# Sevenfold products in units of 512 columns: sums in PSUM banks, and two of four weight sums by accumulating loads

## The chip, the cores and the metric

The kernel runs on one core of one Trainium2 chip. The metric is the device time of one launch in microseconds. The kernel before took 1854.59 us (median of three runs, 1854.23 to 1855.96).

## The reference

Two layers of a decoder trunk, 512 tokens of 1024 channels. Each layer multiplies the normed rows by one wide input matrix, runs five branches (A sparse attention, B latent attention, C differential attention, D spatial gating, E attention into a memory), gates each branch output, projects it, and adds the five projections under a second gate. Cut to what the change touches:

```python
xn = rms_norm(h, norm_g[l])
(..., gates, merge) = jnp.split(xn @ w_in[l], offsets, axis=-1)
gates = gates.reshape(B, S, 5, 512)
merge = merge.reshape(B, S, 5, 1024)
mixed = functools.reduce(jnp.add, [
    sigmoid(merge[:, :, n]) * ((o * silu(gates[:, :, n])) @ w_branch[l, n])
    for n, o in enumerate(branches)])
h = h + mixed @ w_out[l]
```

`gates` of one branch is a product of 1024 x 512 weights with the 512 rows of xn, `merge` one of 1024 x 1024 weights.

## The kernel before, in words

**Arithmetic.** Every dense product is made three times: each operand is a rounded part h and a remainder l, and `three` (L484) adds hh, hl and lh in PSUM, one matmul each (L485 to L487). Weights come in by SyncE's loads into tiles `raw`, ScalarE writes the rounded part `wh` (L371, L402), VectorE or POOL the remainder `wl` (L373, L405). The rows are kept transposed in eight tiles `xh` and `xl`, one for each 128 channels, 512 tokens wide.

**Order of the work.** The kernel is written out by a plan: `ORDER` is a list of tokens, each of which puts units into the plan, and attention runs beside as generators that are advanced by `tick` after each group of matmuls. A unit calls `begin` for each weight granule: that issues the loads of the granules up to four ahead and starts the splits of the next ones; one step of splitting is put in at each `tick`. Instructions are then placed by the program's builder, so that neighbours in the code can change places on an engine.

**The seven stage.** After the token `xs` the last units of a layer (gates of A, merges of A, gates of C, merges of C) use seven products of half blocks in place of eight. The weight block of 1024 channels x 256 columns is cut into four blocks a11, a21 (first column half, upper and lower channels) and a12, a22, each 512 channels x 128 columns; the rows are cut into four as well, and `x_prep` makes their sums t1 to t4. A unit `unit_s` (L509) is 256 columns: it runs products "11", "t2", "t3", "t1", "22", "t4", "21" in that order, each 4 channel tiles x 3 matmuls of 128x256 into a PSUM bank of its own. VectorE adds these up into two tiles `st` (L528), seven times 128x256 a unit; ScalarE copies the first (L526). There are 12 such units a layer, and after each merge unit follows one branch product (24 matmuls of 512 columns, tiles `pm`).

**Weights of the seven stage.** `gseven` loads a unit's block as two `raw` tiles of 512 KB. `seven_steps` (L363) makes four sums of blocks on POOL (`comb`, L380, tiles `ws`, 128x512), and splits the seven operands: `wh` on ScalarE, `wl` on VectorE, the second operand's on POOL. `raw` has four buffers of its own.

**Gate and merge.** A gate unit ends with tanh on ScalarE (L1373), a multiply on VectorE (L1374), a multiply with the branch output on POOL (L1375) and the split into `yh`, `yl`. A merge unit ends with tanh (L1414), VectorE's multiply-add with the branch product (L1403) and POOL's addition into `acc` (L1411).

Of the kernel before, what the change touches and what calls it, by code (L numbers as in the profile page):

```python
# [40 lines left out]
WSB = True  # L41
STB = True
# [15 lines left out]
class Pace:  # L58
    """Interleaves side streams (attention) with the dense products as they are traced."""
# [68 lines left out]
class Granule:  # L128
    """Up to four 128-row blocks of 256 columns of a weight, split in two fp32r parts."""

    def __init__(self, parts, n, width=256, raws=1):
        self.parts, self.n, self.width, self.raws = parts, n, width, raws


def trunk(tc, d, out, taps=None):
# [43 lines left out]
    def f32(ap):  # L179
        return ap.bitcast(F32)  # L180
# [13 lines left out]
    # ---- input rows, small vectors, constants  # L194
# [59 lines left out]
    # ---- rotary tables  # L254
# [42 lines left out]
    def rope(eng, x, j, ct, st, outs=None):  # L297
        """x [128, 2, h, 2H], token tiles 2j and 2j+1; rotated in place or into outs."""
# [19 lines left out]
    # ---- differential lambdas  # L318
# [20 lines left out]
    # ---- long lived tiles  # L339
# [23 lines left out]
    def seven_steps(g):  # L363
        """Seven combinations of the four 512 x 128 blocks of a granule, split, in the order of their products."""
        r0, r1 = g.raw
        a11, a21, a12, a22 = (r[:, :, c * 128:(c + 1) * 128] for r in (r0, r1) for c in range(2))
        g.prod = []

        def put(src):
            h, lo = (z.rearrange("p (k c) -> p k c", k=4) for z in wtile())  # L370
            A.activation(h, src, AF.Copy)  # L371
            yield
            (G if len(g.prod) in GSET else V).tensor_tensor(out=lo, in0=src, in1=f32(h), op=ALU.subtract)  # L373
            g.prod.append((h, lo))
            yield

        def comb(x, y, op):
            o = (blk(F32, "ws") if WSB else pp.tile([128, 512], F32, tag="p", name="ws")).rearrange(
                "p (k c) -> p k c", k=4)
            G.tensor_tensor(out=o, in0=x, in1=y, op=op)  # L380
            return o
        yield from put(a11)
        s1 = comb(a21, a22, ALU.add)
        s2 = comb(s1, a11, ALU.subtract)
        yield from put(s2)
        yield from put(comb(a11, a21, ALU.subtract))
        yield from put(s1)
        yield from put(comb(a12, s2, ALU.subtract))
        yield from put(a22)
        yield from put(a12)  # L390

    def split_steps(g):
        if g.raws == 2:
            yield from seven_steps(g)
            return
        g.raw = g.raw[0]
        g.h, g.l = [], []
        for a in range(0, g.n, 2):
            b = min(a + 2, g.n)
            h, lo = (z.rearrange("p (k c) -> p k c", k=2) for z in wtile())  # L400
            raw, hv, lv = g.raw[:, a:b, :g.width], h[:, :b - a, :g.width], lo[:, :b - a, :g.width]
# [46 lines left out]
    def gseven(w, c0):  # L448
        def parts(*raws):
            return [(r, w[k0 * 128:(k0 + 4) * 128, c0:c0 + 256].rearrange("(k p) c -> p k c", p=128))  # L450
                    for r, k0 in zip(raws, (0, 4))]
        g = Granule(parts, 4, 256, 2)
        order.append(g)
        return g
# [29 lines left out]
    def three(o, ah, al, bh, bl, st, sp):  # L484
        T.matmul(o, ah, bh, start=st, stop=False)  # L485
        T.matmul(o, ah, bl, start=False, stop=False)  # L486
        T.matmul(o, al, bh, start=False, stop=sp)  # L487

    def unit_t(gs, kts, rh, rl, evac, n=512, ms=2):
        """[cols, tokens]: column tiles of 128."""  # L490
# [9 lines left out]
    def unit_n(gs, kts, lh, ll, evac, nt=4):  # L500
        """[tokens, cols]: token tiles in pairs, 256 columns."""
# [7 lines left out]
    def unit_s(g, xb, evac):  # L509
        """Transposed 256 columns by 512 tokens in seven products of half blocks instead of eight."""  # L510
        def run():
            begin(g)
            th = [blk(F32, "st0"), blk(F32, "st1")] if STB else [tr(name="st0"), tr(name="st1")]
            c11, c12, c21, c22 = (t_[:, a:a + 256] for t_ in th for a in (0, 256))
            uses = {"11": [(c11, None)], "t2": [(c22, c11)], "t3": [(c21, c22)], "t1": [(c12, c22), (c22, c21)],
                    "22": [(c12, c12)], "t4": [(c21, c21)], "21": [(c11, c11)]}
            for n, b in enumerate(uses):
                o = psm("s7")[:, :256]
                while len(g.prod) <= n:
                    split_some()  # L520
                for kt in range(4):
                    three(o, g.prod[n][0][:, kt], g.prod[n][1][:, kt], *xb(b, kt), kt == 0, kt == 3)
                    tick(3 * 256 * 0.43)
                for dst, other in uses[b]:
                    if other is None:
                        A.activation(dst, o, AF.Copy)  # L526
                    else:
                        V.tensor_tensor(out=dst, in0=o, in1=other, op=ALU.add)  # L528
            evac(th)
        plan.append(run)  # L530
# [13 lines left out]
    # ---- norm of rows into transposed parts  # L544
# [3 lines left out]
    def norm_rows(rows, ss, gname, l, hi, lo, step=600.0):  # L548
        """rows: [128, 1024] tiles with their sums of squares; writes hi/lo[k] [128, 128 * len(rows)]."""
# [27 lines left out]
    # ---- attention  # L577
# [27 lines left out]
    def pv_causal(o, terms):  # L605
        """terms(kb) -> list of (stationary, part of P)."""
# [8 lines left out]
    def attend(steps, scores, norm, trans, pv, pv_rows=None):  # L615
        """steps: list of (unit, i, last); software pipelined over the steps."""
# [46 lines left out]
    # ================= layers  # L663
# [20 lines left out]
    def layer(l, mm):  # L684
# [5 lines left out]
        # -- memory keys and values  # L690
# [18 lines left out]
        # -- e_q, transposed, one head per column tile  # L709
# [73 lines left out]
        # -- columns 512:1636 in natural layout  # L783
# [114 lines left out]
        # -- latent attention operands  # L898
# [116 lines left out]
        # -- sparse attention  # L1015
# [109 lines left out]
        # -- differential attention, two of its four heads at a time  # L1125
# [93 lines left out]
        # -- spatial gating  # L1219
# [106 lines left out]
        # -- combinations of the half blocks of the normed rows  # L1326
        def x_prep():
            S["t2"] = [c4(F32R, "t2").rearrange("p (k c) -> p k c", k=4) for _ in range(2)]
            for n in ("t3", "t4"):
                S[n] = [[blk(name=n).rearrange("p (k c) -> p k c", k=2) for _ in range(2)] for _ in range(2)]  # L1330
            S["t1"] = [blk(F32, "t1f").rearrange("p (k c) -> p k c", k=2) for _ in range(2)]
            for k in range(4):
                f1, f2 = tr(name="xf1"), tr(name="xf2")
                G.tensor_tensor(out=f1, in0=f32(xh[k]), in1=f32(xl[k]), op=ALU.add)
                V.tensor_tensor(out=f2, in0=f32(xh[k + 4]), in1=f32(xl[k + 4]), op=ALU.add)
                t1 = S["t1"][k // 2][:, k % 2]
                V.tensor_tensor(out=t1, in0=f1[:, 256:], in1=f1[:, :256], op=ALU.subtract)
                V.tensor_tensor(out=f1[:, 256:], in0=f2[:, 256:], in1=f1[:, 256:], op=ALU.subtract)
                V.tensor_tensor(out=f1[:, :256], in0=f2[:, 256:], in1=t1, op=ALU.subtract)
                V.tensor_tensor(out=f2[:, :256], in0=f2[:, :256], in1=f1[:, :256], op=ALU.subtract)  # L1340
                split(S["t2"][0][:, k], S["t2"][1][:, k], f1[:, :256])
                split(S["t3"][0][k // 2][:, k % 2], S["t3"][1][k // 2][:, k % 2], f1[:, 256:])
                split(S["t4"][0][k // 2][:, k % 2], S["t4"][1][k // 2][:, k % 2], f2[:, :256])
# [6 lines left out]
        def xb(b, kt):  # L1350
            if b == "t2":
                return S["t2"][0][:, kt], S["t2"][1][:, kt]
            if b in ("t3", "t4"):
# [5 lines left out]
        # -- gate, project, merge  # L1359
# [3 lines left out]
        def gates(nm, us, seven=False):  # L1363
            bi = "ABCDE".index(nm)

            def ev(ps, u):
                if u == 0:
                    y["h"] = [c4(F32R, "yh").rearrange("p (k c) -> p k c", k=2) for _ in range(2)]
                    y["l"] = [c4(F32R, "yl").rearrange("p (k c) -> p k c", k=2) for _ in range(2)]
                for m in range(2):  # L1370
                    k = 2 * u + m
                    th, sg = tr(name="th"), tr(name="sg")
                    A.activation(th, ps[m], AF.Tanh, scale=0.5)  # L1373
# [234 lines left out]
```

## Time and profile before

| | |
|---|---|
| median of three runs | 1854.59 us |
| profiled execution, span | 1854.6 us |
| TensorE busy | 1784.2 us, 11481 matmuls |
| VectorE busy | 1280.2 us |
| ScalarE busy | 1000.2 us |
| POOL busy | 730.9 us |
| mean granted TensorE clock | 0.986 |
| seven stage, layer 0 | 693.1 to 887.4 us |
| seven stage, layer 1 | 1603.8 to 1801.6 us |

The profiled execution's span equals the median of the runs. PE is TensorE, DVE VectorE, ACT ScalarE, SP SyncE; PEld is TensorE's weight load beside the matmuls. A matmul's row shows a duration that overlaps the next: its cost is the distance from start to start. Brackets behind a row of the timeline are the idle time of that engine before it and what ended it. The clock is a share of full speed. In the names of groups the buffer numbers are left out, so `s` is any bank of a seven product, `pm` any bank of another product. A load's time is from the start of its issue to its landing.

### The profile page before, as it was taken

The page shows a single profiled execution, that of the slowest core. Times are in us where ns is not written, and L with a number is a line of the kernel's source. Part 1 is how long each engine was busy: PE and PEld are TensorE (multiplying, and loading weights), DVE is VectorE, ACT ScalarE, POOL GpSimd, SP SyncE. Part 2 cuts the span into 40 slices and gives each one's busy share as a digit, 9 for nine tenths or more (in the row PEclk, how much of TensorE's full clock was granted, in tenths as well). Part 3 has the DMA queues.
Part 4 walks back from the last instruction along what each step waited for, and adds up shares of the span by engine and source line. Part 5 has one row for each costly group of instructions (what it writes and reads, how often), then busy time and mean ns, then how long its engine had stood idle before and what let it go on. Part 6 is the DMA issues. An engine that isn't in the chain of part 4 may idle for free. (4 is left out here: it accounts for less than half of the span.)

```text
span 1854.6 us, 31211 instructions
## 1 busy us (share of the span) xinstructions
PE 1784.2 (96%) x11481; PEld 1613.9 (87%) x11481; DVE 1280.2 (69%) x2979; ACT 1000.2 (54%) x2247; POOL 730.9 (39%) x603
## 2 busy tenths in 40 slices
PE   7999999999999997999999999999999999899898
PEld 6998889889988777989999988898999887789888
DVE  7438656996755679899354477489775655998963
ACT  7447766437745434455355567653476454444443
POOL 4123111442312366885241321125341133778733
PEclk9999999999999998999999999999999999999999
DMA  6322222332222222334452332223322222233241
GB/s 211 92 69 78 86 69 69 97 97 70 58 58 69 80 58 69 99 95 136 131 177 58 75 89 79 57 80 103 103 58 58 58 80 58 59 91 109 85 148 69
DMA packets 167745, 161.43 MB, mean 87 GB/s; under 512 B 26036, under 2 KB 163304, under 8 KB 167592
## 3 DMA queue, kind: packets, MB, share of 16 engines
q1 hardware_dynamic: 164648, 149.21, 28.0%
q0 software_dynamic: 2944, 10.23, 1.6%
q8 instruction: 91, 1.49, 0.3%
q14 instruction: 62, 0.51, 0.1%
HBM read 155.22 MB, written 4.19 MB: 86 GB/s over the span
## 5 line engine op out<-in xcount | busy, mean ns | idle before, releaser
L405 POOL TENSOR_TENSOR wl<-raw,wh 128x512 fp32r<-128x512 f32 (+1 forms) x226 | 300.8, 1332 | 803.8 <-ACT wh L402 632.8
L402 ACT ACTIVATE wh<-raw 128x512 fp32r<-128x512 f32 (+1 forms) x460 | 285.3, 623 | 328.1 <-PE pm L486 161.6
L485 PE MATMUL pm<-wh,xh 128*128 128x256 f32 x1024 | 294.6, 288 | 0.9 <-ACT nat L1091 0.8
L486 PE MATMUL pm<-wl,xh 128*128 128x256 f32 x1024 | 293.3, 286 | 0.0
L487 PE MATMUL pm<-wh,xl 128*128 128x256 f32 x1024 | 293.2, 286 | 0.0
L405 DVE TENSOR_TENSOR wl<-raw,wh 128x512 fp32r<-128x512 f32 (+1 forms) x234 | 182.7, 782 | 144.5 <-ACT wh L402 140.1
L485 PE MATMUL pm<-xh,wh 128*128 128x512 f32 x656 | 259.2, 396 | 0.8 <-ACT mth L1392 0.5
L487 PE MATMUL pm<-xh,wl 128*128 128x512 f32 x656 | 256.9, 394 | 0.0
L486 PE MATMUL pm<-xl,wh 128*128 128x512 f32 x656 | 256.7, 391 | 0.0
L485 PEld LDWEIGHTS pm<-wh,xh 128*128 128x128 f32 x1024 | 195.1, 190 | 5.8 <-ACT nat L1091 1.6
L487 PEld LDWEIGHTS pm<-wh,xl 128*128 128x128 f32 x1024 | 195.2, 191 | 2.8 <-issue 1.7
L486 PEld LDWEIGHTS pm<-wl,xh 128*128 128x128 f32 x1024 | 195.3, 191 | 2.7 <-issue 1.2
L586 ACT ACTIVATE p<-p,nm 128x512 f32<-128x512 f32 (+1 forms) x192 | 107.2, 558 | 78.2 <-DVE nm L584 77.3
L485 PEld LDWEIGHTS pm<-xh,wh 128*128 128x128 f32 x656 | 123.7, 189 | 26.8 <-ACT mth L1392 1.1
L487 PEld LDWEIGHTS pm<-xh,wl 128*128 128x128 f32 x656 | 123.6, 188 | 26.5
L486 PEld LDWEIGHTS pm<-xl,wh 128*128 128x128 f32 x656 | 123.7, 189 | 23.8
L485 PE MATMUL s<-xh,wh 128*128 128x256 f32 x384 | 113.1, 295 | 25.2 <-ACT mth L1392 12.2
L485 PE MATMUL pm<-yh,wh 128*128 128x512 f32 x320 | 125.9, 394 | 5.3 <-DVE st L528 5.3
L486 PE MATMUL pm<-yl,wh 128*128 128x512 f32 x320 | 126.0, 394 | 0.0
L487 PE MATMUL pm<-yh,wl 128*128 128x512 f32 x320 | 122.6, 392 | 0.0
L486 PE MATMUL s<-xl,wh 128*128 128x256 f32 x384 | 111.4, 290 | 0.0
L487 PE MATMUL s<-xh,wl 128*128 128x256 f32 x384 | 110.6, 291 | 0.0
(378 smaller groups left out, 4756.5 us busy)
## 6 DMA issues: line engine op xcount, KB each, us to landing
raw<-w_in SPq DMA_DIRECT2D x192, 512.0 KB, 3.7
raw<-w_branch SPq DMA_DIRECT2D x40, 512.0 KB, 3.5
raw<-mem_w_kv SPq DMA_DIRECT2D x16, 512.0 KB, 5.6
raw<-w_out SPq DMA_DIRECT2D x16, 512.0 KB, 3.7
raw<-mla_w_uq SPq DMA_DIRECT2D x18, 128.0 KB, 2.7
xrow<-x SPq DMA_DIRECT2D x4, 512.0 KB, 7.9
raw<-mla_w_ukv SPq DMA_DIRECT2D x16, 128.0 KB, 2.7
h<-x POOLq DMA_DIRECT2D x4, 512.0 KB, 4.6
```

Of the source, the lines that this page charges most:

```text
L402: A.activation(hv, raw, AF.Copy)
L405: (G if a else V).tensor_tensor(out=lv, in0=raw, in1=f32(hv), op=ALU.subtract)
L485: T.matmul(o, ah, bh, start=st, stop=False)
L486: T.matmul(o, ah, bl, start=False, stop=False)
L487: T.matmul(o, al, bh, start=False, stop=sp)
L586: A.activation(p[:, :L], p[:, :L], AF.Exp, bias=nm, scale=scale, accum_out=s)
```

## The change

Units of 512 columns take the place of units of 256: six a layer (tokens `oA pA0 pA1 oC pC0 pC1`). The half blocks are 512 channels x 256 columns, loaded as one `raw` of 512 KB each. A product is 4 channel tiles x 2 column halves x 3 matmuls of 128x256, both halves into one PSUM bank of 512, so the count of matmuls is the same as before. Products that go into the same output are added up in the bank: three banks X, Y, Z take the seven products 11, 21, t2, t1, t3, 22, t4, and at six points the bank so far is copied or added into the tiles `st`: three copies on ScalarE, three operations of 128x512 on VectorE, in place of 14 of 128x256 on VectorE and two copies for two units of 256. The code's order has signs changed to fit (`x_prep` makes t1 and t2 with the other sign).

The weight sums: s1 = a21 + a22, s2 = s1 + a11, t3's operand a21 + a11, and s4 = s2 + a12 (signs are in the rows' sums). With `COMB = "part"`, s1 and t3's operand are loads: SyncE loads the first block, and a second load, issued on POOL's queue with `accum_op=ALU.add`, adds the other block onto it (`issue_adds`, called in `begin`). s2 and s4 are made on VectorE, in two pieces each. All 14 remainders `wl` of a unit are made on VectorE. A unit loads seven times 512 KB where two units before loaded four times.

`raw` has no buffers of its own any more: it takes them from the pool `c4` (12 where there were 6); the pool `blk` has 34 in place of 36, and t2 moved there. `x_prep` runs wholly on VectorE.

```diff
-         "gD0 gD1 +df1 mD0 mD1 -df1 mD2 xp mD3 !xp xs gA0 gA1 mA0 mA1 mA3 mA2 gC0 gC1 mem mC0 mC1 mC3 mC2")
+         "gD0 gD1 +df1 mD0 mD1 -df1 mD2 xp mD3 !xp xs oA pA0 pA1 oC mem pC0 pC1")
-NB = 36
-NC4 = 6
+NB = 34
+NC4 = 12
-NRAW = 4
-GSET = (1,)
+COMB = "part"
...
-            g.raw = [wp.tile([128, 4, 256], F32, tag="raw", bufs=NRAW, name="raw") for _ in range(g.raws)]
+            g.raw = [c4(name="raw").rearrange("p (k c) -> p k c", k=4) for _ in range(g.raws)]
...
+    def issue_adds(k):
+        for g in order[k:min(k + 5, state["dma"])]:
+            n = len(g.adds)
+            while g.added < n and order.index(g) <= k + 1 + n - g.added:
+                dst, src = g.adds[g.added]
+                nc.gpsimd.dma_start(dst(), src, accum_op=ALU.add)
+                g.added += 1
...
-    def seven_steps(g):
...
-            (G if len(g.prod) in GSET else V).tensor_tensor(out=lo, in0=src, in1=f32(h), op=ALU.subtract)
...
-            G.tensor_tensor(out=o, in0=x, in1=y, op=op)
...
-            (G if a else V).tensor_tensor(out=lv, in0=raw, in1=f32(hv), op=ALU.subtract)
+            (G if a and g.sums is None else V).tensor_tensor(out=lv, in0=raw, in1=f32(hv), op=ALU.subtract)
...
         issue(k + 4)
+        issue_adds(k)
         split_upto(k + 2)
...
+        elif COMB == "part":
+            def s2(p):
+                o = add(fresh("s2", p), pc("s1", p), pc("a11", p))
...
+            def load_s1(raw):
+                U["s1"] = raw
+                return [(raw, a22)]
...
+            def s4(p):
+                o = add(U["s2", p], U["s2", p], pc("a12", p))
...
+            gs = [one("a11", a11), one("a12", a12),
+                  made(s2, load_s1, 1, [((lambda: U["s1"]), a21)]), made(s1),
+                  one("t3", None, a21, [a11]), made(s4), one("a22", a22)]
...
+    def unit_o(gs, xb, evac):
+        def run():
+            th = [c4(F32, "st").rearrange("p (m t) -> p m t", m=2) for _ in range(2)]
...
+            steps = [("X", "11", copy(c11)), ("Y", "21", plus(c11)), ("X", "t2", copy(c12)), ("Z", "t1", copy(c22)),
+                     ("X", "t3", neither(c22)), ("Z", "22", plus(c12)), ("X", "t4", None)]
+            for g, (bk, b, post) in zip(gs, steps):
+                begin(g)
+                new = bk not in bank
+                if new:
+                    bank[bk] = psm("s7")
+                o = bank[bk]
+                for kt in range(4):
+                    for m in range(2):
...
+                        tick(3 * 256 * 0.47)
+                o = o.rearrange("p (m t) -> p m t", m=2)
+                if post is not None:
+                    post(o)
+                evac(b, th, o)
...
-                G.tensor_tensor(out=f1, in0=f32(xh[k]), in1=f32(xl[k]), op=ALU.add)
+                V.tensor_tensor(out=f1, in0=f32(xh[k]), in1=f32(xl[k]), op=ALU.add)
...
+        def gates_o(nm):
+            def ev(b, th, o):
+                if b == "22":
+                    for m in range(2):
+                        gated(nm, m, th[0][:, m])
+                elif b == "t4":
+                    A.activation(th[1][:, :, :256], o, AF.Copy, scale=-1.0)
+                    for m in range(2):
+                        gated(nm, 2 + m, th[1][:, m])
+            unit_o(goct(w, C_GATE + 512 * "ABCDE".index(nm)), xb, ev)
```

POOL's order in layer 0 of the kernel before, in the gate units of A and the start of the merge units (`ws` are the sums, `sg` the gate multiplications, `wl` second operands or second halves of splits, `acc` the multiply-adds of the branches):

```order
L380 TENSOR_TENSOR ws<-raw 128x512
L380 TENSOR_TENSOR ws<-ws,raw 128x512
L380 TENSOR_TENSOR ws<-raw 128x512
L1375 TENSOR_TENSOR sg<-sg,oA 128x512 x2
L380 TENSOR_TENSOR ws<-raw,ws 128x512
L373 TENSOR_TENSOR wl<-ws,wh 128x512
L1375 TENSOR_TENSOR sg<-sg,oA 128x512 x2
L380 TENSOR_TENSOR ws<-raw 128x512
L380 TENSOR_TENSOR ws<-ws,raw 128x512
L380 TENSOR_TENSOR ws<-raw 128x512
L405 TENSOR_TENSOR wl<-raw,wh 128x512
L380 TENSOR_TENSOR ws<-raw,ws 128x512
```

In the changed kernel the same place, from the last splits of the branch before to the first multiply-adds of A (a DMA row is an accumulating load onto a `raw`):

```order
L383 TENSOR_TENSOR wl<-raw,wh 128x512
L1483 TENSOR_TENSOR acc<-acc,mth 128x512 x2
L362 DMA raw<-w_in 128x4x256
L1446 TENSOR_TENSOR sg<-sg,oA 128x512 x4
L362 DMA raw<-w_in 128x4x256 x3
L383 TENSOR_TENSOR wl<-raw,wh 128x512 x2
L1483 TENSOR_TENSOR acc<-acc,st 128x512 x4
L362 DMA raw<-w_in 128x4x256
L383 TENSOR_TENSOR wl<-raw,wh 128x512 x2
L362 DMA raw<-w_in 128x4x256
L749 DMA memrow<-mem 128x512 x4
```

The sums and the splits of the seven operands are gone. The first load row is that for t3 in the gate unit; the three behind the four multiplications are s1 and t3 of the first merge unit and s1 of the second.

VectorE's order at the end of A's gate units before (`yl` are remainders of the gated branch, `st` the sums out of PSUM):

```order
L188 TENSOR_TENSOR yl<-sg,yh 128x512
L528 TENSOR_TENSOR st_8639<-s_8714,st_8639 128x256
L528 TENSOR_TENSOR st_8638<-s_8733,st_8638 128x256
L373 TENSOR_TENSOR wl<-ws,wh 128x512
L528 TENSOR_TENSOR st_8639<-s_8747,st_8639 128x256
L373 TENSOR_TENSOR wl<-ws,wh 128x512
L528 TENSOR_TENSOR st_8638<-s_8761,st_8638 128x256
L373 TENSOR_TENSOR wl<-ws,wh 128x512
L1374 SCALAR_TENSOR_TENSOR sg<-th,st_8638 128x512
```

And in the changed kernel, where `s_8774` and `s_8789` are the two pieces of s2 and then of s4, in the first merge unit:

```order
L1445 SCALAR_TENSOR_TENSOR sg<-th,st 128x512
L186 TENSOR_TENSOR yl<-sg,yh 128x512 x2
L584 TENSOR_TENSOR st<-s_8770,st 128x2x256
L186 TENSOR_TENSOR yl<-sg,yh 128x512
L451 TENSOR_TENSOR s_8774<-raw 128x512
L451 TENSOR_TENSOR s_8789<-raw 128x512
L383 TENSOR_TENSOR wl<-raw,wh 128x512 x2
L383 TENSOR_TENSOR wl<-s_8774,wh 128x512
L383 TENSOR_TENSOR wl<-s_8789,wh 128x512
```

The sums out of PSUM that stood between the splits are one row; behind it the sums of weight blocks come first and the splits of s1 and s2 after them.

## Rows read from the trace of the kernel before

**Rows 1.** Stretches: us, busy and count by engine, clock, DMA share, GB/s

```profile
693.10:887.40 194.30, 176.57 (x1219) 166.26 (x1218) 171.31 (x243) 95.54 (x179) 138.01 (x95) 0.95 0.34 102
887.40:1603.80 716.40, 712.11 (x4525) 638.41 (x4523) 461.69 (x1225) 397.56 (x931) 220.48 (x189) 1.00 0.29 83
1603.80:1801.60 197.80, 174.47 (x1203) 164.18 (x1202) 169.53 (x227) 90.07 (x162) 136.31 (x89) 0.95 0.32 94
```

**Rows 2.** Timeline, TensorE, 256 columns: start, us, engine, line, operation, tiles

```profile
719.79 0.28 PE L486 MATMUL s<-xl,wh 128*128 128x256 f32 x1
...
720.03 0.28 PE L485 MATMUL s<-xh,wh 128*128 128x256 f32 x1
```

**Rows 3.** Timeline, TensorE, 512 columns, up to the next form

```profile
748.19 0.39 PE L485 MATMUL pm<-yh,wh 128*128 128x512 f32 x1
...
748.87 0.28 PE L487 MATMUL s<-xh,wl 128*128 128x256 f32 x1
```

**Rows 4.** Waits of TensorE, layer 0's stage: us in total, times, longest

```profile
PE s L485 <- DVE st L528: 7.3, 5, 3.5
PE s L485 <- ACT mth L1392: 6.1, 1, 6.1
PE s L485 <- DVE mth L1403: 2.4, 1, 2.4
PE pm L485 <- DVE st L528: 1.7, 1, 1.7
```

**Rows 5.** Waits of TensorE, layer 1's stage

```profile
PE s L485 <- DVE st L528: 9.8, 5, 3.0
...
PE pm L485 <- DVE st L528: 3.6, 2, 3.2
```

**Rows 6.** One stretch after a stall, columns as in rows 1

```profile
819.90:825.80 5.90, 5.90 (x28) 5.90 (x29) 5.80 (x10) 3.31 (x9) 2.39 (x2) 0.50 0.39 139
```

**Rows 7.** Groups, layer 0's stage: count, busy us, mean ns, idle before

```profile
L373 DVE TENSOR_TENSOR wl<-raw,wh 128x512 fp32r<-128x512 f32 x36 | 44.8, 1247 | 0.1
...
L380 POOL TENSOR_TENSOR ws<-raw 128x512 f32<-128x512 f32 x22 | 36.3, 1652 | 7.8 <-DMA raw<-w_in 7.8
L528 DVE TENSOR_TENSOR st<-s,st 128x256 f32<-128x256 f32 x84 | 33.6, 414 | 4.6 <-PE s L487 4.1
...
L380 POOL TENSOR_TENSOR ws<-raw,ws 128x512 f32<-128x512 f32 x12 | 20.0, 1669 | 1.6 <-DVE acc L1406 1.6
L373 POOL TENSOR_TENSOR wl<-ws,wh 128x512 fp32r<-128x512 f32 x12 | 18.5, 1545 | 7.3 <-ACT wh L371 7.3
L380 POOL TENSOR_TENSOR ws<-ws,raw 128x512 f32<-128x512 f32 x11 | 17.3, 1574 | 0.8
```

**Rows 8.** Timeline, VectorE, a split while POOL is idle

```profile
729.32 0.68 DVE L373 TENSOR_TENSOR wl<-ws,wh 128x512 fp32r<-128x512 f32 x1
```

**Rows 9.** Timeline, ScalarE, end of the second gate unit of A

```profile
731.29 1.15 ACT L1373 ACTIVATE th<-st 128x512 f32<-128x512 f32 x2 [4.14 <-DVE st L528]
```

**Rows 10.** Timeline, POOL, the same unit's last multiplications

```profile
732.73 3.37 POOL L1375 TENSOR_TENSOR sg<-sg,oA 128x512 f32<-128x512 f32 x2 [5.48 <-DVE sg L1374]
```

**Rows 11.** Timeline, POOL, multiply-adds of the branch before the stage

```profile
705.33 2.98 POOL L1411 TENSOR_TENSOR acc<-acc,mth 128x512 f32<-128x512 f32 x2 [1.23 <-DVE mth L1403]
```

**Rows 12.** Loads issued from 640 to 890: count, KB, median us to landing

```profile
raw<-w_in SPq DMA_DIRECT2D x26, 512.0 KB, 3.7
...
h<-x POOLq DMA_DIRECT2D x4, 512.0 KB, 4.6
memrow<-mem POOLq DMA_DIRECT2D x4, 256.0 KB, 5.8
```

**Rows 13.** Timeline, POOL, four issues of loads

```profile
815.32 2.24 POOL L672 DMA_DIRECT2D memrow<-mem  x4
```

**Rows 14.** Loads issued from 815.8 to 816.1, columns as in rows 12

```profile
raw<-w_in SPq DMA_DIRECT2D x1, 512.0 KB, 8.0
```

More of the change, by code (lines that the diff above doesn't have):

```diff
@@ L128, with __init__ @@
 class Granule:
-    def __init__(self, parts, n, width=256, raws=1):
+    def __init__(self, parts, n, width=256, raws=1, adds=(), sums=None):
         self.parts, self.n, self.width, self.raws = parts, n, width, raws
+        self.adds, self.added, self.sums = adds, 0, sums
 def trunk(tc, d, out, taps=None):
@@ L482, in unit, with three @@
         plan.append(run)
[L484 to L487, printed above, removed]
+    def three(o, ah, al, bh, bl, st, sp, shared=False):
+        T.matmul(o, ah, bh, start=st, stop=False, skip_group_check=shared)
+        T.matmul(o, ah, bl, start=False, stop=False, skip_group_check=shared)
+        T.matmul(o, al, bh, start=False, stop=sp, skip_group_check=shared)
     def unit_t(gs, kts, rh, rl, evac, n=512, ms=2):
@@ L1384, in merges, with gated @@
-        def merges(nm, us, last=False, seven=False):
-            bi = "ABCDE".index(nm)
+        def gated(nm, k, src):
+            if k == 0:
+                y["h"] = [c4(F32R, "yh").rearrange("p (k c) -> p k c", k=2) for _ in range(2)]
+                y["l"] = [c4(F32R, "yl").rearrange("p (k c) -> p k c", k=2) for _ in range(2)]
+            th, sg = tr(name="th"), tr(name="sg")
+            A.activation(th, src, AF.Tanh, scale=0.5)
+            V.scalar_tensor_tensor(out=sg, in0=th, scalar=1.0, in1=src, op0=ALU.add, op1=ALU.mult)
+            G.tensor_tensor(out=sg, in0=sg, in1=oT[nm][k], op=ALU.mult)
+            split(y["h"][k // 2][:, k % 2], y["l"][k // 2][:, k % 2], sg)
@@ new lines, in merged @@
+        def merged(k, th, ps, last):
+            first = acc[k] is None
+            if first:
+                acc[k] = blk(F32, "acc")
+            dst = acc[k] if first else th
+            V.scalar_tensor_tensor(out=dst, in0=th, scalar=1.0, in1=ps, op0=ALU.add, op1=ALU.mult)
+            if first:
+                return
+            if last:
+                V.tensor_tensor(out=acc[k], in0=acc[k], in1=dst, op=ALU.add)
+                M.setdefault("h", {})[k] = blk(name="mxh")
+                M.setdefault("l", {})[k] = blk(name="mxl")
+                split(M["h"][k], M["l"][k], acc[k])
+            else:
+                G.tensor_tensor(out=acc[k], in0=acc[k], in1=dst, op=ALU.add)
@@ new lines, in merges, with merges_o, ev @@
+                branch(nm, u, th, False)
+        def merges_o(nm, p, last):
+            ths = [{}, {}]
+            def ev(b, th, o):
+                if b == "t3":
+                    A.activation(th[1][:, :, 256:], th[1][:, :, 256:], AF.Tanh, scale=0.5)
+                elif b == "22":
+                    A.activation(th[0], th[0], AF.Tanh, scale=0.5)
+                elif b == "t4":
+                    A.activation(th[1][:, :, :256], o, AF.Tanh, scale=-0.5)
+                    for j in range(2):
+                        for m in range(2):
+                            ths[j][m] = th[j][:, m]
+            unit_o(goct(w, C_MERGE + 1024 * "ABCDE".index(nm) + 512 * p), xb, ev)
+            for j in range(2):
+                branch(nm, 2 * p + j, ths[j], last)
@@ L1456, in layer @@
             elif c == "g":
-                gates(a[0], (int(a[1]),), seven)
+                gates(a[0], (int(a[1]),))
             elif c == "m":
-                merges(a[0], (int(a[1]),), seven=seven, last=a[0] == "C")
+                merges(a[0], (int(a[1]),))
+            elif c == "o":
+                gates_o(a)
+            elif c == "p":
+                merges_o(a[0], int(a[1]), a[0] == "C")
+            elif tok == "xp":
+                do(lambda: pace.later(0.0, x_prep(), "xp"))
+            elif tok == "xs":
+                do(x_swap)
             elif tok == "qr":
```

223 lines of the change are left out of this document (104 added, 119 removed).

## The prediction

> **What bounds the kernel now.** I read the stretches first. TensorE is the bound nearly everywhere: between the two stretches that this change rewrites it is busy 712.11 of 716.40 us, and the two "seven stages" themselves take 194.30 and 197.80 us with TensorE at 0.95 of its clock [rows 1]. So I ask what those stages lose. Matmuls follow one another every 0.12 us at 256 columns (0.24 us for two) and every 0.227 us at 512 (0.68 us for three) [rows 2, 3]. A stage has 12 units of 84 matmuls of 256 columns, 1008 x 0.12 = 121.0 us, and eight branch products of 24 of 512, 192 x 0.227 = 43.6 us: 164.6 us. In the first layer the transposes of the memory rows, 16 small ones at an estimated 0.14 us, add 2.2. The stages lose 194.3 - 166.8 = 27.5 and 197.8 - 164.6 = 33.2 us, together 61. Everything the change can give is in these 61 us, less than 3.3% of 1854.6.
>
> The waits say where they lie: in layer 0 TensorE stands 17.5 us, 9.0 of it for VectorE's sums of products out of PSUM (L528), 6.1 for ScalarE's last tanh before the stage, 2.4 for the multiply-add behind it [rows 4]; in layer 1 those sums cost 9.8 + 3.6 = 13.4 us [rows 5], and the row of the tanh stands there word for word again. Most of the other 20 us is clock: after a stall the granted clock is 0.50, the lower level of 1.2 GHz, and 28 matmuls took 5.90 us where 28 x 0.12 = 3.36 were due, 2.5 us given away [rows 6]. So a stall of a few us costs itself and some 2.5 us more; two shorter ones often share one such stretch.
>
> **What the change removes.** POOL's sums of weight blocks (45 rows worth 73.6 us in layer 0) and its twelve second splits (18.5 us) go [rows 7]: 92 of its 138 us. VectorE loses 84 small sums (33.6 us) [rows 7] and gets 18 of 512 columns, some 13 us if one is 0.75, plus 24 sums of weight blocks and twelve more splits at 0.68 us uncontended [rows 8], 24 us. It has splits at a mean of 1.25 us [rows 7] against 0.68 because POOL works beside it; with POOL's work down by two thirds most come near 0.7, and 36 of these alone give back up to 20 us. VectorE, 171.31 us busy of 194.30 [rows 1], falls to some 150: it gets no harder bound. The waits for L528 (9.0 + 13.4 us) therefore go, and with them some 10 us of lower clock. The 6.1 us at the stage's start go mostly as well: the first product needs one PSUM bank whose last reader comes early, and the next needs only plainly loaded blocks.
>
> No matmul is added or taken: 6 x 168 = 12 x 84. The extra loads, 3 x 0.52 MB for each of 12 units, are 19 MB in 392 us, 48 GB/s on top of 102 and 94, and a DMA share of 0.34 becomes about 0.5 [rows 1]: room is left. Work moved to VectorE ahead of the stage (four additions of 0.7 us) lies under a TensorE busy 99% there [rows 1]; uncovered it would cost 2.8 us.
>
> **What it adds: two waits for an accumulating load.** The lifetimes of PSUM banks no longer matter; the arrival of two sums does. TensorE does products 11 and 21, then waits for the splits of s2 (second in line among the sums) and of s1, both from s1, which is a22 loaded by SP and a21 added onto it by a load on POOL's queue. Before, the first sum was POOL's own addition, 1.65 us from two landed blocks [rows 7]. Now the order shows POOL's loads for the merge unit behind four gate multiplications of the unit just ended, and what stands behind that load on VectorE is its sums and five splits.
>
> The gate chain's length is in the trace: a tanh began at 731.29, as soon as VectorE's last sum was there [rows 9], and POOL's second multiplication ended at 732.73 + 3.37 = 736.10, 4.8 us on [rows 10]. Put 0.6 for the copy out of PSUM before it (a tanh of this size is 1.15 / 2 [rows 9]), and POOL is free T + 5.4 us, T being the end of the gate unit's last product. TensorE has 46 matmuls left by then, 46 x 0.12 = 5.5 us. The load lands L after its issue, then come ScalarE's split or VectorE's two sums, and one VectorE split, 3 x 0.68 [rows 8] and handoffs: 2.3. TensorE is idle for 5.4 + L + 2.3 - 5.5 = L + 2.2; to that 2.6 us of lower clock after it [rows 6], and 1 us because product t3 comes right behind t2 in the same bank X and waits for its copy. **L + 5.8 us, four times** (after the gates of A and C, in both layers).
>
> At the stage's start (twice) the order has t3's load behind POOL's last two multiply-adds of the stage before. VectorE's multiply-adds stand behind the splits of product 21, at about 4.4 us, then 1.35, then 2.98 on POOL [rows 11]: issue at 8.8. It lands at 8.8 + L, is split 1.5 later, and TensorE is there after 96 x 0.12 = 11.5 us and an estimated 1.5 of waiting for s2's split. So idle L - 2.6, plus 1.5, plus about 2.0 for the clock: **L + 0.9, twice**. Small waits for copies and plain loads: 3. Sum after: 4(L + 5.8) + 2(L + 0.9) + 3 = **6L + 28**, against 61; it breaks even at L = 5.5.
>
> **The price L.** No accumulating load is in this trace. The nearest rows: a plain load of the same 512 KB by SP 3.7, by POOL 4.6, four 256 KB loads of POOL in this very stage 5.8 [rows 12]; an SP load that met these, 8.0 [rows 14]. An accumulating load moves the destination too; twice 4.6 is 9.2. Less than 3.7 I exclude: it moves no fewer bytes than that load. I take **L = 6**, nearest to the POOL row from this stage, and one that meets SP's loads as these will. Then 6 x 6 + 28 = 64: 3 us lost, 1854.6 + 3 = **1858 us** (the profiled span, 1854.6, is the median of the runs too). At 3.7 the loss is 50 (1844); at 8.0 it is 76, and since the other loads for t3 have a slack of some 6.5 us each, eight of them would be 1.5 late: 88 (1882).
>
> Beside SP's load meeting POOL's: the rows show POOL's four issues back to back, 2.24 us in all [rows 13], while VectorE was at work. The Trainium skill ("SBUF — State Buffer", SBUF: two separate sides) says that loads from the GpSimd queue have descriptors written by GpSimd, which VectorE's two-port operations shut out. By that rule each of the six loads on the path would start up to one VectorE operation later, some 0.7 to 1.8 us, and the sum would be 4 to 11 us higher; the trace does not show it in the issue times, so the forecast has none of it. The skill's fit for such a load ("DMA: Bandwidth & Descriptors", Anatomy of one DMA — SWDGE) gives, as an estimate, 2.0 + 1.2 = 3.2 us for 512 KB, without the accumulation; POOL's row above is 4.6, and the measurement decides.
>
> **The rivals.** *A: the accumulating load lands like a plain one,* 3.7 to 5. For it: the DMA engines are loaded to a third [rows 1] and 4.6 is the median of POOL's own loads. Against it: the adding, and 5.8 in this stage. 50 to 58 lost: 1844 to 1852, faster. *B: it is slow,* L from 7 up, as with loads that meet (8.0) or twice the bytes (9.2). Its place is the first sum after each gate unit; it decides from 6.1, where the loss passes the measurement's bound; at 8.0 1882, at 9.2, with t3 late by 2.7 eight times, 6 x 9.2 + 28 + 22 = 105, 1899. Slower. *C: the boundary is shorter than I make it,* because with the sums gone from POOL, VectorE's gate operations take 0.7, POOL's 1.3 to 1.4, so that its last multiplication is out at T + 3.7: four times 1.7 less at the same L, and where L is near 4.6 a shorter stretch of lower clock as well: 6 x 4.6 + 28 - 7 - 4 = 45, 1839. Against it: splits of the next unit still stand between them. *D: VectorE becomes the bound,* if its 128x512 operations stay at 1.25 us: 12 + 24 more of them and 13 of sums, 58 us against 33.6 saved, make 171 + 25 = 196 us of work in a stage; with some 9 us of waits, 205 against 194 and 198, 18 in all: 1873. The two thirds of POOL's work that go speak against it.
>
> **How the numbers follow.** Forecast (stalls change place, L 5 to 7, 58 to 70 lost, 1852 to 1864): 0.40. A: 0.28. B: 0.16. C: 0.12. D: 0.04. A run can tell 0.2%, 3.7 us, from no change: 1850.9 to 1858.3. Faster needs a loss under 57.3, L under 4.9: nearly all of A and all of C, 0.38. The same needs L between 4.9 and 6.06: half of the forecast's own case and a little of A, 0.22. Slower: the other half, B and D, 0.40. The range goes from 1837 (C) to 1885 (B at 8); outside are B's upper part and the best of C. The likeliest case by itself: 1852 to 1864.
>
> **What would show it.** In the profile after: no row of waits for sums out of PSUM above 2 us in all (right) or as now (D); at each gate-to-merge boundary one TensorE gap of 7 to 9 us released by the split of s1 or s2 (right), 5 to 6 (A, C), over 9 (B), and a clock near 0.5 behind it; POOL's accumulating load issued 5 to 6 us after the gate unit's last matmul, its landing giving L directly; a gap of 3 to 4 us before t3 at both stage starts; splits on VectorE at a mean of about 0.75. The forecast is wrong as a mechanism if these boundaries have no gap, or if the time lies outside the two stages.

## The result, and the profile after

The changed kernel took 1868.20 us (median of four runs, 1865.68 to 1869.56) against 1855.28 for the kernel before: a ratio of 1.0072, 95% interval 1.0060 to 1.0084. It is slower by some 13 us. The forecast was 1858 with a range of 1837 to 1885, likeliest 1852 to 1864; slower had a chance of 0.40, faster 0.38. The profiled execution was the fastest of the four: 1865.68 us, of which 1863.9 are the span and 1.8 lie around it.

The stretches of the profile after, cut where the seven products of a layer begin and where its output projection begins, with the columns of [rows 1]:

```profile
690.30:890.40 200.10, 174.60 (x1218) 163.41 (x1217) 135.69 (x197) 97.33 (x171) 60.19 (x49) 0.96 0.55 137
890.40:1608.10 717.70, 712.18 (x4526) 638.85 (x4525) 460.09 (x1245) 402.35 (x943) 210.03 (x182) 1.00 0.29 85
1608.10:1811.10 203.00, 175.11 (x1201) 164.06 (x1200) 130.72 (x181) 92.19 (x154) 57.17 (x44) 0.93 0.53 130
```

The stages are 5.8 and 5.2 us longer than those of [rows 1], the stretch between them is 1.3 longer, and the first stage begins 2.8 us sooner. The engines did what the edit says: VectorE falls from 171.31 to 135.69 us busy, POOL from 138.01 to 60.19. VectorE's splits, which took 1247 ns each in [rows 7], now have a mean of 744, and its sums of weight blocks 765 and 846:

```profile
L383 DVE TENSOR_TENSOR wl<-raw,wh 128x512 fp32r<-128x512 f32 x67 | 49.1, 744 | 30.4 <-ACT wh L380 30.1
...
L451 DVE TENSOR_TENSOR s<-s,raw 128x512 f32<-128x512 f32 x12 | 10.0, 846 | 0.1
L451 DVE TENSOR_TENSOR s<-raw 128x512 f32<-128x512 f32 x12 | 8.8, 765 | 14.3 <-DMA raw<-w_in 14.3
```

The last row shows the price: VectorE itself stood 14.3 us for loads. All waits of TensorE in layer 0's stage after, to be held against [rows 4]:

```profile
PE s L547 <- ACT wh L380: 24.8, 10, 8.9
PE s L549 <- DVE wl L383: 0.7, 3, 0.2
```

and in layer 1's, where [rows 5] stood:

```profile
PE s L547 <- ACT wh L380: 27.4, 10, 8.8
PE s L549 <- DVE wl L383: 0.4, 2, 0.2
```

No wait for a sum out of PSUM is left, nor the 6.1 us for the tanh. In their place are ten waits a layer for a split, 8.9 us the longest. One of these is at the end of A's gate unit in layer 0. The last matmul of that unit, then POOL, VectorE (one row while POOL multiplies, one behind the load) and TensorE in the timeline after:

```profile
712.84 0.28 PE L549 MATMUL s<-t,wl 128*128 128x256 f32 x1
...
714.80 3.38 POOL L1446 TENSOR_TENSOR sg<-sg,oA 128x512 f32<-128x512 f32 x2 [1.23 <-DVE sg L1445]
718.80 1.64 POOL L1446 TENSOR_TENSOR sg<-sg,oA 128x512 f32<-128x512 f32 x1 [0.62 <-DVE sg L1445]
720.39 2.61 POOL L362 DMA_DIRECT2D raw<-w_in  x2
...
716.95 1.77 DVE L1445 SCALAR_TENSOR_TENSOR sg<-th,st 128x512 f32<-128x512 f32 x1
726.52 1.29 DVE L451 TENSOR_TENSOR s<-raw 128x512 f32<-128x512 f32 x2 [4.34 <-DMA raw<-w_in]
...
727.21 0.58 PE L547 MATMUL s<-xh,wh 128*128 128x256 f32 x1 [8.57 <-ACT wh L380]
```

The accumulating load of s1 is issued when the fourth multiplication ends, 7.4 us after the end of the unit's last matmul (712.84 + 0.12); it lands 6.1 us later, and only then VectorE and ScalarE can begin; TensorE stands 8.57 us. The block that it adds onto had been asked for by SyncE 30 us earlier:

```profile
690.46 0.37 SPq L353 DMA_DIRECT2D raw<-w_in  x1
```

A stretch of the lower clock follows such a gap as before, here behind the second of the four, 31 matmuls in 6.90 us at 0.54 (columns of [rows 1]). Behind the first a stretch of the same length had a mean of 0.75 and 42 matmuls. The row of the second:

```profile
826.70:833.60 6.90, 6.63 (x31) 6.34 (x32) 5.54 (x10) 3.27 (x6) 0.00 (x0) 0.54 0.82 206
```

The loads from 690 to 890 after, columns of [rows 12]: the eleven accumulating ones have a median of 7.2 us, POOL's plain ones 3.8.

```profile
raw<-w_in SPq DMA_DIRECT2D x23, 512.0 KB, 4.0
raw<-w_in POOLq DMA_DIRECT2D x11, 512.0 KB, 7.2
...
h<-x POOLq DMA_DIRECT2D x4, 512.0 KB, 3.8
```

### The profile page after: what moved, and what is told of

Same layout as the page of the kernel before. It is cut to its first block, busy times and chain, and to the rows that moved or that the text cites. A ratio compares the mean times of both kernels' runs of the same rounds, so it can differ in the third digit from the quotient of the medians.

```text
span 1863.9 us, 30974 instructions
## 1 busy us (share of the span) xinstructions
PE 1780.8 (96%) x11481; PEld 1610.2 (86%) x11481; DVE 1202.9 (65%) x2927; ACT 1012.1 (54%) x2253; POOL 552.7 (30%) x499
## 5 line engine op out<-in xcount | busy, mean ns | idle before, releaser
L380 ACT ACTIVATE wh<-raw 128x512 fp32r<-128x512 f32 (+1 forms) x580 | 359.4, 624 | 440.1 <-PE pm L548 192.2
L383 DVE TENSOR_TENSOR wl<-raw,wh 128x512 fp32r<-128x512 f32 (+1 forms) x354 | 262.1, 746 | 210.2 <-ACT wh L380 207.3
L547 PE MATMUL pm<-wh,xh 128*128 128x256 f32 x1024 | 294.5, 288 | 0.9 <-ACT nat L1168 0.8
L547 PE MATMUL pm<-xh,wh 128*128 128x512 f32 x656 | 258.2, 394 | 0.5 <-ACT mth L1500 0.5
L547 PEld LDWEIGHTS pm<-wh,xh 128*128 128x128 f32 x1024 | 195.1, 191 | 5.6 <-ACT nat L1168 1.6
L547 PE MATMUL s<-xh,wh 128*128 128x256 f32 x384 | 113.2, 295 | 38.6 <-ACT wh L380 38.6
L547 PEld LDWEIGHTS pm<-xh,wh 128*128 128x128 f32 x656 | 123.2, 188 | 26.3 <-ACT mth L1500 1.1
L547 PE MATMUL pm<-yh,wh 128*128 128x512 f32 x320 | 124.6, 392 | 0.5 <-ACT mth L1500 0.5
L547 PEld LDWEIGHTS s<-xh,wh 128*128 128x128 f32 x384 | 77.0, 200 | 40.9 <-ACT wh L380 40.6
```

The source lines that it names most:

```text
L383: (G if a and g.sums is None else V).tensor_tensor(out=lv, in0=raw, in1=f32(hv), op=ALU.subtract)
L547: T.matmul(o, ah, bh, start=st, stop=False, skip_group_check=shared)
```

## The experiments

**One: the load ahead of the multiplications.** POOL's order is changed so that the load of s1 stands before the four gate multiplications.

```diff
-            while g.added < n and order.index(g) <= k + 1 + n - g.added:
+            while g.added < n and order.index(g) <= k + 3 + n - g.added:
...
+                    with tc.issue_after(state["add"].ins):
+                        for f in held:
+                            f()
                         for m in range(2):
                             gated(nm, 2 + m, th[1][:, m])
```

(`held` are the first two multiplications and their splits, kept until then.)

> The changed kernel with one thing moved: POOL issues the accumulating load of s1 for the merge unit ahead of the four gate multiplications instead of behind them; nothing is added or left out. Theory (the load's place in POOL's queue makes the gap): both loaded blocks are there 9 us before the issue, so the load is issued about 8 us earlier and the four gaps of 8.4 to 8.9 us after the gate units shrink to 1 to 2 us, most of the lower clock behind them goes too: 1868 - 4 x 7.2 - 5 = about 1834 us. Rival (the gap is VectorE's and ScalarE's chain of sums and splits behind the load, or the bank X): the load comes earlier but the gaps stay within 1 to 2 us of what they were: 1860 to 1868. Second rival (the earlier load meets SyncE's loads and takes 9 us instead of 6): gaps of 4 to 5, about 1848.

Measured: 1855.31 us, ratio to before 1.0001 (0.9989 to 1.0013): 13 us less than the changed kernel, a good third of what the theory expected. The load was issued at 699.96 and landed at 707.92, 7.96 us later but long before it was needed (so the second rival's reason falls, though its gap of 4 to 5 us is what came), and yet TensorE stands again in the same place. TensorE and VectorE of that run:

```profile
725.91 0.39 PE L549 MATMUL s<-xh,wl 128*128 128x256 f32 x1 [4.56 <-DVE wl L383]
```

```profile
719.41 0.68 DVE L1445 SCALAR_TENSOR_TENSOR sg<-th,st 128x512 f32<-128x512 f32 x1
720.01 0.68 DVE L186 TENSOR_TENSOR yl<-sg,yh 128x512 fp32r<-128x512 f32 x1
720.61 1.77 DVE L1445 SCALAR_TENSOR_TENSOR sg<-th,st 128x512 f32<-128x512 f32 x1
722.30 0.68 DVE L383 TENSOR_TENSOR wl<-s,wh 128x512 fp32r<-128x512 f32 x1
722.91 1.75 DVE L186 TENSOR_TENSOR yl<-sg,yh 128x512 fp32r<-128x512 f32 x1
724.58 0.68 DVE L383 TENSOR_TENSOR wl<-s,wh 128x512 fp32r<-128x512 f32 x1
725.18 0.68 DVE L383 TENSOR_TENSOR wl<-raw,wh 128x512 fp32r<-128x512 f32 x1
```

The split that TensorE waits for (725.18) stands on VectorE behind the gate chain, whose operations take 0.68 us alone and 1.77 beside POOL's multiplications. So both the theory and its rival hold a part: the queue on POOL made 4 of the 8.5 us, and a second wait lay hidden behind it. (The earlier load also put two of VectorE's sums into the gate chain, 2.4 us; experiment four shows the same wait without that.)

**Two: the price of adding.** The loads on POOL's queue as plain loads over the block; the two sums are left out of what this kernel computes.

```diff
-                nc.gpsimd.dma_start(dst(), src, accum_op=ALU.add)
+                nc.gpsimd.dma_start(dst(), src)
```

> The changed kernel with its second loads on POOL's queue as plain loads, not added onto the block but written over it; this leaves the sums s1 and that of t3 out of the computation. It prices the adding alone. Theory: POOL's plain load of 512 KB took 3.5 to 4.0 us in this trace, the accumulating ones 6.0 to 9.7, so each gap after a gate unit shrinks by 2.2 us and the late t3 of the merge units (10.9 us in all) goes: 1868 - 9 - 11 - 2 = about 1846 us. Rival (what costs is the issue on POOL and its place in the queue, the adding is free): landing times stay at 6 us, 1862 to 1870.

Measured: 1841.59 us, ratio 0.9924 (0.9904 to 0.9944), against 1846 expected. The same eleven loads land in 4.9 us at the median instead of 7.2:

```profile
raw<-w_in POOLq DMA_DIRECT2D x11, 512.0 KB, 4.9
```

The four gaps shrink to 6.6 to 6.8 us, and the waits for t3 are gone: 16.0 us of waits in layer 0, seven times, where there were 24.8.

```profile
PE s L547 <- ACT wh L380: 16.0, 7, 6.8
```

The adding as such costs 27 us here; the rival falls.

**Three: the gate multiplications on VectorE, in all units.**

```diff
-            G.tensor_tensor(out=sg, in0=sg, in1=oT[nm][k], op=ALU.mult)
+            V.tensor_tensor(out=sg, in0=sg, in1=oT[nm][k], op=ALU.mult)
```

> The changed kernel with the gate multiplications (and those of the other branches' gates) on VectorE in place of POOL, so that nothing stands ahead of the load in POOL's queue. Theory of the queue: the load goes out as soon as its block is there, and the gaps after the gate units shrink from 8.5 to 1 to 3 us as in the kernel with the load moved ahead: 1835 to 1842 us (four multiplications of 0.7 us more on VectorE come before the sums of weight blocks there). Rival (VectorE's chain makes the gap): the gap stays or grows by up to 2.8 us: 1868 to 1880.

Measured: 1849.71 us, ratio 0.9974 (0.9963 to 0.9986). The gap after the gate units is 1.6 us and a second of 1.1 follows, as the theory has it and not its rival; the two stages lost 24 us against the changed kernel.

```profile
727.11 0.39 PE L547 MATMUL s<-xh,wh 128*128 128x256 f32 x1 [1.64 <-ACT wh L380]
```

The time misses both all the same: the rest of the profiled execution was 11.6 us longer. The other branches' gates had their multiplications moved as well; experiment five asks whether that is why.

**Four: no accumulating load, all four sums on VectorE.**

```diff
-COMB = "part"
+COMB = "dve"
```

> The changed kernel with no accumulating load: all four sums of weight blocks on VectorE (eight additions of 128x512 a unit in place of four), everything loaded by SyncE. It has the 512-column units with products added up in PSUM alone. Theory: what the units give stays (no waits for sums out of PSUM), what the loads cost goes: 45 us after the gate units, 5 at the stage starts and 11 of late t3, less some 10 to 15 of new waits for VectorE's sums: about 1820 us, 1812 to 1832. Rival (VectorE becomes the bound with 14 splits and eight sums a unit, or the units themselves cost time): 1850 or more.

Measured: 1853.35 us, ratio 0.9987 (0.9975 to 0.9998). The theory misses by more than 20 us and the rival's number (1850 or more) holds: with neither the loads nor the sums out of PSUM, the kernel is 0.1% from where it was before. Whether the rival's reason holds is for experiment six. VectorE and TensorE after A's gate units:

```profile
727.89 0.68 DVE L186 TENSOR_TENSOR yl<-sg,yh 128x512 fp32r<-128x512 f32 x1
728.49 0.68 DVE L451 TENSOR_TENSOR s<-raw 128x512 f32<-128x512 f32 x1
729.20 0.69 DVE L451 TENSOR_TENSOR s<-s,raw 128x512 f32<-128x512 f32 x1
...
729.88 0.58 PE L547 MATMUL s<-xh,wh 128*128 128x256 f32 x1 [4.87 <-ACT wh L380]
```

All blocks had landed; the first sum (728.49) stands behind the last remainder of the gate chain (727.89). It is the second wait of experiment one, seen without the first: 3.8 to 4.9 us at the four places.

**Five: as three, in the seven stage alone.**

```diff
-        def gated(nm, k, src):
+        def gated(nm, k, src, E=G):
...
-            G.tensor_tensor(out=sg, in0=sg, in1=oT[nm][k], op=ALU.mult)
+            E.tensor_tensor(out=sg, in0=sg, in1=oT[nm][k], op=ALU.mult)
...
-                        gated(nm, m, th[0][:, m])
+                        gated(nm, m, th[0][:, m], V)
...
-                        gated(nm, 2 + m, th[1][:, m])
+                        gated(nm, 2 + m, th[1][:, m], V)
```

> The changed kernel with the gate multiplications on VectorE in the two gate units of the seven stage alone; the other branches' gates keep theirs on POOL. In the kernel with all of them moved, the two stages were 23.8 us shorter in the profile than in the changed kernel (222.8 + 222.9 against 233.3 + 236.2 from the last spatial product to the output projection) and the rest 11.6 us longer. Theory (the rest is the price of the other gates' multiplications on VectorE): 1868 - 24 = 1844 us. Rival (the rest's 11.6 us are scatter of short stretches of lower clock, and come back): 1850 as with all moved.

Measured: 1844.67 us, ratio 0.9949 (0.9933 to 0.9964): the theory's number. Against experiment three the medians differ by 5.0 us and the parts of the profiles outside the two stages by 8.7, so the other gates' multiplications account for 5 to 9 of those 11.6 us. They belong on POOL.

**Six: four and five together.**

> All four sums of weight blocks on VectorE and no accumulating load, and the gate multiplications of the seven stage on VectorE too. In the kernel with the sums alone on VectorE TensorE stood 3.8 to 4.9 us after each gate unit because the sums were queued on VectorE behind the gate chain, whose remainders wait for POOL's multiplications of 1.7 us each. Theory (it is this lockstep of VectorE and POOL): the gaps fall to 1 to 2 us, 1853 - 4 x 3.5 - 5 of lower clock = 1834 us. Rival (VectorE's amount of work, 14 splits and eight sums a unit, makes the gaps): four multiplications more leave them where they are or longer, 1850 to 1860.

Measured: 1841.51 us, ratio 0.9928 (0.9910 to 0.9947): 12 us less than four, of the 19 expected. The gap falls to 1.64 us, but one of 1.8 us for VectorE's next split follows it:

```profile
724.05 0.39 PE L547 MATMUL s<-xh,wh 128*128 128x256 f32 x1 [1.64 <-ACT wh L380]
...
727.19 0.58 PE L549 MATMUL s<-xh,wl 128*128 128x256 f32 x1 [1.84 <-DVE wl L383]
```

Taken together the waits at this place fall from 5.2 us in experiment four (4.87 and 0.35) to 3.8 (1.64, 0.30 and 1.84). So theory and rival hold a part each: the lockstep of VectorE with POOL (each waits for the other's result in turn) made 3.2 us of the one gap, and 1.8 us of new waiting for VectorE's splits take the place of more than half of them. In the profiles the stages are 7.5 us shorter; the other 4 of the 12 us lie outside them and are not explained.

**Seven: t3's sum on VectorE, s1 by the accumulating load as in the changed kernel.**

```diff
+            def load_t3(raw):
+                U["t3"] = raw
+                return [(raw, a21)]
+
+            def t3(p):
+                o = add(pc("t3", p), pc("t3", p), pc("a11", p))
+                yield
+                return o
...
-                  one("t3", None, a21, [a11]), made(s4), one("a22", a22)]
+                  made(t3, load_t3, 1), made(s4), one("a22", a22)]
```

> The changed kernel with one of its two accumulating loads taken away: t3's operand is a21 loaded by SyncE and a11 added by VectorE; s1 stays an accumulating load behind POOL's gate multiplications. Theory (t3's late landing cost 8.9 us of gaps and 2 of lower clock in the merge units and the gates of C, and 5 at the stage starts): 1868 - 16 + 1 to 3 for two additions a unit = 1852 to 1855 us, the four gaps of 8.4 to 8.9 us stay. Rival (t3's operand is late because its base or its place in the order is, not the adding load): 1863 to 1870.

Measured: 1855.65 us, ratio 1.0004 (0.9993 to 1.0015), against 1852 to 1855. The four gaps stay (8.4 to 8.5 us), and the waits for t3 go, as the rows of layer 0 show (L556 and L590 are L547 and L581 of the changed kernel):

```profile
PE s L556 <- ACT wh L380: 19.4, 7, 8.5
PE s L556 <- ACT st L590: 2.6, 2, 1.4
```

So the second accumulating load cost some 13 us of the changed kernel's time by itself.

**Eight: five and seven together.**

> Both: t3's sum on VectorE, and the seven stage's gate multiplications on VectorE, with s1 alone an accumulating load, which then has nothing ahead of it on POOL. Theory (the gaps after the gates are POOL's queue and VectorE's lockstep with it, the late t3 are the second load): 1844 - 13 of gaps - 4 of lower clock = 1827 us, less than both kernels. Rival (with more on VectorE its queue becomes the wait): 1840 or more.

Measured: 1830.30 us, ratio 0.9869 (0.9853 to 0.9885): less than both kernels, and 3 us above the theory. Its waits in layer 0's stage and in layer 1's:

```profile
PE s L556 <- ACT wh L380: 7.6, 7, 1.8
PE s L556 <- ACT st L590: 2.6, 2, 1.4
```

```profile
PE s L556 <- ACT wh L380: 7.4, 7, 1.6
PE s L556 <- ACT st L590: 2.9, 3, 1.3
```

Twenty us of waits where there were 53. The gate chain on VectorE has no row above 0.69 us an operation any more; it ends 7.0 us after the gate unit's last matmul, where it took 9.2 in the changed kernel with four operations fewer on VectorE. The sums of the next unit start right behind it, at 722.14. TensorE's gap there is 1.64 us; s1 had long landed, and its split (721.28) stood on ScalarE behind the rounded parts of the gate chain:

```profile
718.95 1.28 DVE L1455 TENSOR_TENSOR sg<-sg,oA 128x512 f32<-128x512 f32 x2
720.33 1.29 DVE L186 TENSOR_TENSOR yl<-sg,yh 128x512 fp32r<-128x512 f32 x2
721.54 0.68 DVE L593 TENSOR_TENSOR st<-s,st 128x512 f32<-128x512 f32 x1
722.14 1.28 DVE L451 TENSOR_TENSOR s<-raw 128x512 f32<-128x512 f32 x2
...
721.95 0.38 PE L556 MATMUL s<-xh,wh 128*128 128x256 f32 x1 [1.64 <-ACT wh L380]
```

**Nine: the kernel before with the same move.** Its units of 256 columns, with the seven stage's multiplications on VectorE.

```diff
-                    G.tensor_tensor(out=sg, in0=sg, in1=oT[nm][k], op=ALU.mult)
+                    (V if seven else G).tensor_tensor(out=sg, in0=sg, in1=oT[nm][k], op=ALU.mult)
```

> The kernel before (units of 256 columns, sums on POOL and VectorE) with the gate multiplications of its seven stage on VectorE, nothing else. It tells whether the 25 us that the last kernel gains on before come from that move alone. Theory (before's stalls are VectorE's 84 small sums queued behind contended splits; POOL keeps its sums, VectorE is 88% busy there and gets 8 operations more): within 5 us of before, 1850 to 1860. Rival (the lockstep of VectorE with POOL's multiplications is as costly there): the nine stalls for sums after the gate units shrink by half or more, 1840 to 1846.

Measured: 1867.38 us, ratio 1.0070 (1.0046 to 1.0095): slower by 12 us, outside what either expected. The move that takes 24 us off the changed kernel costs the one before 12. Waits of TensorE in layer 0's stage there, against [rows 4] (a fourth, 2.4 us for the multiply-add, is as before), and the moved multiplications of A:

```profile
PE s L485 <- DVE st L528: 9.3, 6, 3.0
PE s L485 <- ACT mth L1392: 6.1, 1, 6.1
PE pm L485 <- DVE st L528: 4.3, 2, 3.5
...
L1375 DVE TENSOR_TENSOR sg<-sg,oA 128x512 f32<-128x512 f32 x4 | 3.8, 953 | 0.0
```

The waits for sums out of PSUM rise from 9.0 to 13.6 us: TensorE waits behind VectorE's queue there, and the move makes that queue longer. The multiplications took 0.95 us each, against 0.68 in experiment eight; POOL still works beside them there, on the weight sums. So the gain of experiment eight needs the new units, which take those sums off POOL and the small ones off VectorE; which of the two counts for more, no run separates.

## Why the prediction was right, and where its sum was off

**What was removed** came out as forecast. The waits for L528 and the tanh are gone, VectorE's busy time fell further than said (135.7 us against "some 150"), its splits to 0.74 against 0.75, and the loss lies inside the two stages: outside them the profiled execution is 1.7 us shorter. Rival D (VectorE as the bound) fell with it, though experiment six shows that it is not far: with all four sums VectorE's queue shows again.

**The boundary after the gate units** was the mechanism: one gap each, behind the split of s1, with the load behind POOL's four multiplications. Forecast 8.2 us of gap at L = 6; the four gaps are 8.57, 8.91, 8.77 and 8.38, the landings 6.1, 6.5, 6.3 and 6.0 us. With the small gaps for bank X and the lower clock behind, the term 4(L + 5.8), 47 us at L = 6, measured 50.5. (Each measured term here is the sum of what its matmuls' starts lie apart beyond 0.12 and 0.227 us.) That the gap came out so near is in part luck, for two steps of its sum were wrong and nearly cancel. POOL was free at T + 7.4 us at all four places, not T + 5.4, so the sign "issued 5 to 6 us after the gate unit's last matmul" failed: three of POOL's four multiplications still ran behind that matmul, in turns with operations of VectorE that took up to 1.78 us. And from the landing to TensorE's start it was 0.7 us, not 2.3: the first matmul that waits is one for s1, which needs ScalarE's split of the loaded block and none of VectorE's sums.

**The stage's start** was put too high: 2(L + 0.9) = 13.8, measured 6.0. The accumulating load of t3 was issued at 696.67, 6.4 us after the first product (690.3), not 8.8, as VectorE's multiply-adds came earlier; no wait for s2's split was there; and the gaps of 1.6 and 2.9 us, where the sign said 3 to 4, were followed by no stretch at 0.50.

**The step that failed in size** is the single price L with a slack of "some 6.5 us each" for the other loads of t3. At 6 us it gave them nothing; measured were 13.3 us in four places, half of it in one gap of 3.73 in layer 1, whose load took 9.7 us, and in the clock behind it:

```profile
1691.38 0.58 PE L547 MATMUL s<-t,wh 128*128 128x256 f32 x1 [3.73 <-ACT wh L380]
```

L is not one number. Alone an accumulating load of 512 KB lands in 5.9 to 6.6 us, with one exception (7.5 at the start of layer 1's stage, beside no other transfer and not explained), the second of a pair in 7.2 to 8.2, and beside SyncE's loads, as in most of the merge units, in 7.8 to 9.7. The prediction had that row, 8.0 for a load that met others [rows 14], and used it only for the other end of the range. In the gate units of C the load took no more than 6.3 and was late all the same, since it was issued late. Experiment seven took t3's accumulating load away, here and at the stage's starts, and got 12.6 us back of the 19 that the two terms make; waits of 2.6 us a layer for the copy out of bank X, which it shows instead, are most of the rest.

**The sum.** 50.5 + 6.0 + 13.3 + 2.7 of small waits = 72.5 us against the forecast's 64 and the 61 before. That is the profiled execution, 9.3 us longer in span than the one of before; the medians stand 12.9 apart. The start, 7.8 us too high, hid more than half of what the loads of t3 were too low, which is luck again; and even so 1868.2 lies above the likeliest case, 1852 to 1864. With 0.40 on slower and 0.38 on faster the direction was hardly forecast. The prediction also took the profiled span of before for a run's time; in the profiled run after, 1.8 us lie outside the span, so the sum should have been made in differences.

**The rivals.** A (a plain load's price) has its answer in experiment two: at a median of 4.9 us the kernel takes 1841.6, below A's 1844 to 1852. C (a short boundary) did not come by itself; experiments one and four show why, and correct the forecast's picture. It counted the gate chain mainly as what delays POOL's load. The same chain holds TensorE up for 3.8 to 4.9 us, through VectorE's next sums and splits, even when every block is there, and the load's wait lay on top of it. By these two runs a smaller L alone could have taken away some half of the gap, no more. B's price was reached by some loads, but its place was t3 in the merge units, not the sum after the gates.

**The rule on shut-out descriptors** (the Trainium skill, "SBUF — State Buffer", SBUF: two separate sides) would, as the prediction applied it, have set the loads later by one VectorE operation each. In the trace the load of s1 is issued as POOL's multiplication ends (718.80 + 1.64 = 720.44 and 720.39), and a load issued at 696.67 with VectorE at work landed after 6.11 us, one at 647.90 with VectorE idle after 6.07. So nothing of the kind is seen. The page says it of VectorE's operations in a two-port mode, and no run shows that the sums and splits at this place are such.

## What to carry to other kernels

Before a sum is moved onto an accumulating load, look at what stands ahead of that load in its queue, and count it as late by that work plus the load plus everything that must still be made from it; then ask for the next wait, which the first one hides. Do not give one price to every transfer: those that met others took up to 1.6 times as long here. Moving one helper operation between two engines was worth minus 24 us in one kernel and plus 12 in another; look first at which engine's queue TensorE waits behind. And check the terms of a sum one by one, also where the sum comes out right.

## What the runs showed of the hardware

Adding onto the destination costs a 512 KB load some 2 us when it is alone (mostly 5.9 to 6.5 in the two stages, against 4.0 to 4.4 on the same queue in experiment two) and more beside others; its issue takes POOL 1.3 us against 0.8. The Trainium skill ("DMA: Bandwidth & Descriptors", Anatomy of one DMA — SWDGE) gives 3.2 us, as an estimate from its fit, for a plain load of this size; POOL's plain ones that were alone measured 3.5 to 4.4, and the measurement decides. A VectorE operation of 128x512 took 0.68 us alone and, at the longest, 1.78 to 1.80 beside POOL, in every run. That factor, and not the number of operations, made the gate chain long: 9.2 us from the unit's last matmul to its last remainder in the changed kernel, 7.0 with four operations more on VectorE and none on POOL (experiments five and eight).
